# Two plain pairs ahead of the Strassen pairs, and a down-projection with five raw weight buffers, an in-place activation split and PSUM banks that rotate over its groups

## The chip, the cores and the metric

The kernel runs on one core of one Trainium2 chip. Its metric is the device time of one execution in microseconds (us); less is better. Times of whole runs are medians of several runs. The profile is one execution taken by the hardware profiler.

## The reference

One inference step of a two-layer encoder over 1024 prompt positions and 8 x 16 sample positions, 1152 rows of 1024 values in float32. Each layer has an attention block and a feed-forward block (ConvFFN), both modulated by vectors computed from c and closed by a layer norm. Layer 0 uses sliding-window attention, layer 1 a chunk band with its own bias table and a K/V projected after layer 0. The part that the change touches is the feed-forward block and the norm after it:

```python
def conv_ffn(h, prev, w_up, conv_w, conv_b, w_down):
    u = h @ w_up                                   # 1024 -> 2 x 2816
    ...
    ue = jnp.concatenate([prev.astype(u.dtype), u], axis=1)
    y = conv_b
    for tap in range(CONV_W):                      # causal depthwise, 3 taps
        y = y + conv_w[tap] * ue[:, tap:tap + T]
    a, g = jnp.split(y, 2, axis=-1)
    out = (jax.nn.gelu(g) * a) @ w_down            # 2816 -> 1024
    return out, ue[:, T:]
...
x = layer_norm(DEEPNORM_ALPHA * x + (1 + g_f) * f, ln_g[l, 1], ln_b[l, 1])
```

## The kernel before, in words

Every float32 matmul is done as three float32r matmuls: each operand is split into a high part (a copy with rounding, on ScalarE, L160) and a low part (the rest, a subtraction on VectorE or GpSimd, L171). H holds the high and low part of the transposed layer input for all 1152 rows (nine tiles of 128). X1 and X2 hold work operands, F is a float32 arena of 12672 columns whose regions are reused by hand, `ws` are two raw weight buffers, `wslots` four slots for split weights. PSUM has eight banks of 512 columns.

The program is written in program order against a scheduler that lays out each engine's instructions ahead of time, by a simulated timeline and with program order as priority. At run time each engine runs its own list in that order, and waits on semaphores where an operand or a buffer is not ready; SyncE (SP) issues all the loads and stores from one list. `self.bg` is background work (the ada vectors of later blocks), advanced by step().

One layer is attention(), out_proj(), ffn(), and at its end down().

*out_proj()* goes over the tiles 8, 0, ..., 7, writes the new transposed input of a tile to H and to hD in DRAM. Its last tiles use hf, xr, tmp, lng and lnb in F.

*ffn()* computes 22 pairs of 128 columns (one of the value half, one of the gate half). The first NPL pairs are *plain*: mmT() for each half and each of three column blocks, 24 matmuls a block, into banks `ub`, with the taps (conv_block) read from PSUM; L1032 copies the last rows of a block. All others are *Strassen pairs* (spair): seven products of half-size operands in place of eight, 24 matmuls each (L1180), read out of PSUM by L1139, L1142 and L1147 into rows `us` of F, on which conv_row() does the taps (L1058, L1019). The weight sums S1, S2, S3 lie at F[0:1536] and are made on GpSimd (L1129 to L1132). Both kinds end in gated(), which stores actD[j]. The rows y come from a ring of three at F[10492], F[6396] and F[7548].

The Strassen products need combined inputs: combine() loads hD tile by tile through a ring of buffers in F, makes the differences on GpSimd (L1087, L1088) and VectorE (L1089, L1090) and splits them into T2, T3, T4 (in X1 and X2); T1S is a float32 region at F[2706:5010], split into H by first(). The first product of a pair needs only H, the second T2, the fourth T3, the fifth T1. During the pairs the raw weights go through `wide`, a ring of the two ws buffers, F[11644:12668] and F[8700:9724]; in layer 0 the background ada loads go through the same ring, and their matmuls (L217) write bank 7.

*down()* computes three groups of three tiles (GR). For each j of 22, fetch() loads a weight row block (L175), splits it into a slot (four slots in layer 0, ten in layer 1, where H is free), loads 384 columns of actD[j] (L1237) into one of three raw buffers at F[0:1152], and splits them into one of twelve slots in X1. mm() adds 6 matmuls per tile (L1246) in banks 2i and 2i+1. tail() multiplies by the gate (L1260, the only reader of the banks), adds the residual loaded by L946, and normalises; in layer 0 the tile is transposed (L904) into banks 6 and 7, scaled (L912, L916), saved (L920) and split into H. Ahead of it layer 0 builds a bias table for layer 1 (tables_b) and writes its skewed copy with one store, skb (skew, L1317). ln_consts() loads the gates and the layer-norm rows, four loads of 512 KB.

The down-projection of layer 0 is followed by attention(1), which begins with vproj(1, 0): nine tiles in the order 0, 1, 2, 6, 7, 8, 3, 4, 5, 24 matmuls each (L302), in banks 0, 1, 2, 3 in turn. rescale() (L801) uses lng and lnb after that.

Of the kernel before, what the change touches and what calls it, by code (L numbers as in the profile page):

```python
# [10 lines left out]
F32 = mybir.dt.float32  # L11
# [21 lines left out]
NPL = 1  # L33
BGU = 0.5
# [62 lines left out]
class Trunk:  # L97
# [742 lines left out]
    def ln_consts(self, l, i):  # L840
        nc = self.nc
        g = self.gd[2 * l + i]
        nc.sync.dma_start(self.gateP, bass.AP(g.tensor, g.offset, [[0, 128], [1, D]]))
        nc.sync.dma_start(self.gateS, bass.AP(g.tensor, g.offset + D, [[D, 8], [0, 16], [1, D]]))
        ln = (2 * l + i) * 2
# [137 lines left out]
    def ffn(self, l, xsrc, xdst, affs):  # L983
# [29 lines left out]
        ub = Ring([0, 1, 2])  # L1013
# [65 lines left out]
        def combine():  # L1079
            ring = Ring([F[:, 1536:2560], F[:, 7548:8572]])  # L1080
            for t in (8, 0, 1, 2, 3, 4, 5, 6, 7):
# [41 lines left out]
        def spair(j):  # L1123
# [46 lines left out]
            for i, (src, q, g, start) in enumerate(plan):  # L1170
# [19 lines left out]
                self.step(BGU)  # L1190
# [20 lines left out]
    def down(self, l, xsrc, xdst, affs):  # L1211
# [10 lines left out]
        self.ln_consts(l, 1)  # L1222
        raw = Ring([F[:, i * 384 : i * 384 + 384] for i in range(3)])
# [6 lines left out]
        tb = Ring([6, 7])  # L1230
# [3 lines left out]
        def fetch(j, t0):  # L1234
            w = self.wload(I["wdn"][l, j])
            s = raw.next()
            nc.sync.dma_start(s, self.actD[j][:, t0 * 128 : t0 * 128 + 384])  # L1237
            a = acts.next()
            self.split(s, *a, "a", "v")
            return w, a  # L1240

        def mm(j, w, a, i):
            for hf in range(2):
                ps = self.bank(2 * i + hf)
# [9 lines left out]
        def tail(t, i):  # L1254
            row, sm = z.next(), self.sm.next()
            x = self.residual(t, xsrc, xr)
            gate = self.gateP if t < 8 else self.gateS
            for hf in range(2):
                n = slice(hf * 512, hf * 512 + 512)
                nc.vector.tensor_mul(row[:, n], self.bank(2 * i + hf), gate[:, n])  # L1260
# [19 lines left out]
        for gi, g in enumerate(GR):  # L1280
            keep = KEEP if l and gi == 2 else 0
            for j in range(NFF - keep):
                w, a = fetch(j, g[0])
                for i in range(3):
                    mm(j, w, a, i)
            if gi == 0:
                aff = affs()
            kept = [(j, *fetch(j, g[0])) for j in range(NFF - keep, NFF)]
            for i, t in enumerate(g):
                for j, w, a in kept:  # L1290
                    mm(j, w, a, i)
                tail(t, i)
        if not l:
            self.wring = Ring(ws)
# [277 lines left out]
```

## Time and profile before

| | |
|---|---|
| median of 3 runs | 2967.39 us (2963.93 to 2974.32) |
| the profiled execution | 2964.33 us, its span 2962.6 us |
| TensorE (PE) busy | 2743.6 us, 93% of the span |
| PE weight loads (PEld) busy | 2432.2 us, 82% |
| VectorE (DVE) busy | 1894.1 us, 64% |
| ScalarE (ACT) busy | 1298.4 us, 44% |
| GpSimd (POOL) busy | 1138.2 us, 38% |
| moved by DMA | 471.17 MB, 159 GB/s on average |
| mean granted TensorE clock | 0.965 |

How to read the rows that follow: in a timeline each row gives the start in us, the duration in us, the engine, the line of the kernel, the operation, what it writes and reads, the shape and a count of instructions merged into the row; the bracket is the idle time of that engine just before, and who ended it. `SPq` is a load or store being issued. Rows of the chain of waits give start, length and what the time went to. Rows that start with a window A:B give its length, then busy time and instruction count of PE, PEld, DVE, ACT and POOL, the granted clock, the DMA engines' share and GB/s.

### The profile page before, as it was taken

To read this page: it belongs to the slowest core of one execution; us is meant where nothing else is said; L and a number is where in the kernel's file an instruction comes from. 1 tells how busy PE (TensorE), PEld (TensorE's weight loads), DVE (VectorE), ACT (ScalarE), POOL (GpSimd) and SP (SyncE) were. 2 spreads that over 40 slices of the span, in tenths; PEclk is the share of its full clock that TensorE was granted. 3 is DMA by queue.
4 is the path that set the end of the run, shared out by engine and by line. 5 is a ranking of instruction groups with operands and counts; after the bars stand their busy time and mean duration, and the time that the engine had idled before them with its cause. 6 is when DMAs were issued, how large, how long until landed. Compare 5 with 4: busy or idle time off the path is not lost.

```text
span 2962.6 us, 47567 instructions
## 1 busy us (share of the span) xinstructions
PE 2743.6 (93%) x17782; PEld 2432.2 (82%) x17782; DVE 1894.1 (64%) x3702; ACT 1298.4 (44%) x2625; POOL 1138.2 (38%) x765
## 2 busy tenths in 40 slices
PE   7999899799999969999998999889889999998987
PEld 5888677699999957778998888758789999986766
DVE  4476777677777756672113677668768877865773
ACT  3466634333333333443325666652434444443442
POOL 2122523334433335664730111322433443336553
PEclk9999899899999989999999999999989999999999
DMA  8654454334444475665964457674422222155552
GB/s 292 206 176 149 151 177 163 122 129 139 137 132 137 128 253 174 220 209 169 299 219 151 125 157 194 185 207 150 150 81 75 67 85 75 53 184 175 191 192 86
DMA packets 221064, 471.17 MB, mean 159 GB/s; under 512 B 39616, under 2 KB 115600, under 8 KB 220832
## 3 DMA queue, kind: packets, MB, share of 16 engines
q1 hardware_dynamic: 220832, 468.13, 49.4%
q8 instruction: 140, 2.29, 0.3%
q14 instruction: 92, 0.75, 0.1%
HBM read 366.74 MB, written 110.74 MB: 161 GB/s over the span
## 4 chain that ended last, share of the span: by engine, by line
PE 67%; DMA 8%; DVE 5%; issue 3%; ACT 2%; POOL 2%; SPq 1%; POOLq 0%; ACTq 0%; DVEq 0%
PE PS L1180 30%; PE PS L1246 13%; PE PS L302 9%; PE PS L290 8%; DMA ws<-in_wdn_dram 3%; PE PS L564 1%; PE PS L586 1%; PE PS L217 1%; DVE xa L171 1%; DMA F<-actD 1%; PE PS L536 1%; POOL H L171 1%; PE PS L539 1%; POOL wl L171 1%; PE PS L904 1%
## 5 line engine op out<-in xcount | busy, mean ns | idle before, releaser
L171 POOL TENSOR_TENSOR wl<-ws,wh 128x1024 fp32r<-128x1024 f32 x136 | 336.5, 2481 | 384.8 <-ACT wh L160 357.0
L1180 PE MATMUL PS<-H,wh 128*128 128x256 f32 (+1 forms) x2688 | 414.3, 297 | 0.0
L171 DVE TENSOR_TENSOR xa<-F,xa 128x384 fp32r<-128x384 f32 (+1 forms) x168 | 271.6, 1628 | 208.2 <-ACT xa L160 196.7
L1246 PE MATMUL PS<-wh,xa 128*128 128x512 f32 x1128 | 362.7, 400 | 39.1 <-ACT wh L160 23.8
L160 ACT CAST wh<-ws 128x1024 fp32r<-128x1024 f32 (+1 forms) x232 | 203.6, 879 | 420.8 <-DMA ws<-in_wdn_dram 152.9
L1180 PEld LDWEIGHTS PS<-H,wh 128*128 128x128 f32 x2688 | 379.3, 191 | 0.0
L1142 DVE TENSOR_TENSOR F<-PS,F 128x320 f32<-128x320 f32 (+2 forms) x630 | 202.3, 351 | 142.2 <-PE PS L1180 139.0
L1246 PEld LDWEIGHTS PS<-wh,xa 128*128 128x128 f32 x1128 | 214.2, 190 | 93.0 <-ACT wh L160 24.6
L1019 DVE SCALAR_TENSOR_TENSOR F<-F 128x1024 f32<-128x1024 f32 x336 | 264.8, 826 | 35.7 <-ACT F L1058 35.4
L1180 PE MATMUL PS<-H,wl 128*128 128x320 f32 (+1 forms) x1344 | 244.0, 301 | 27.6 <-ACT H L160 25.0
L290 PE MATMUL PS<-H,wh 128*128 128x384 f32 (+1 forms) x1344 | 262.2, 340 | 0.0
L160 ACT CAST wh<-F 128x512 fp32r<-128x512 f32 x202 | 124.1, 622 | 278.8 <-PE PS L1180 169.7
L171 DVE TENSOR_TENSOR wl<-F,wh 128x512 fp32r<-128x512 f32 x202 | 201.4, 1004 | 58.1 <-ACT wh L160 57.8
L290 PEld LDWEIGHTS PS<-H,wh 128*128 128x128 f32 x1344 | 236.9, 191 | 1.4 <-issue 1.0
L1180 PEld LDWEIGHTS PS<-H,wl 128*128 128x128 f32 x1344 | 200.4, 192 | 43.5 <-ACT H L160 25.7
L1246 PE MATMUL PS<-wl,xa 128*128 128x512 f32 x564 | 225.5, 400 | 5.0 <-POOL wl L171 4.8
L1180 PE MATMUL PS<-xa,wh 128*128 128x320 f32 (+1 forms) x1344 | 207.4, 297 | 0.2 <-DVE xa L171 0.2
L1028 POOL TENSOR_TENSOR F<-F 128x16 f32<-128x16 f32 x88 | 39.8, 453 | 410.3 <-DVE F L1019 336.2
L1180 PEld LDWEIGHTS PS<-xa,wh 128*128 128x128 f32 x1344 | 189.4, 190 | 0.6 <-DVE xa L171 0.6
L1246 PE MATMUL PS<-H,xa 128*128 128x512 f32 x684 | 167.1, 405 | 20.5 <-DVE F L1260 13.2
L302 PE MATMUL PS<-wh,H 128*128 128x256 f32 (+1 forms) x936 | 170.3, 311 | 7.1 <-DVE H L171 3.8
L1246 PEld LDWEIGHTS PS<-H,xa 128*128 128x128 f32 x684 | 132.2, 194 | 54.2 <-issue 13.6
(242 smaller groups left out, 5516.2 us busy)
## 6 DMA issues: line engine op xcount, KB each, us to landing
ws<-in_wdn_dram SPq DMA_DIRECT2D x132, 512.0 KB
ws<-in_adaw_dram SPq DMA_DIRECT2D x62, 512.0 KB
F<-in_adaw_dram SPq DMA_DIRECT2D x50, 512.0 KB
ws<-in_wup_dram SPq DMA_DIRECT2D x50, 512.0 KB
actD<-F SPq DMA_DIRECT2D x44, 576.0 KB
F<-actD SPq DMA_DIRECT2D x132, 192.0 KB
F<-in_wup_dram SPq DMA_DIRECT2D x38, 512.0 KB
xa<-kH SPq DMA_DIRECT2D x60, 256.0 KB
```

The source lines that it names most:

```text
L160: nc.scalar.copy(out, in_)
L171: self.eng(el).tensor_sub(lo, src, hi.bitcast(F32))
L217: mm = nc.tensor.matmul(ps[32 * j : 32 * j + 32, hf * 256 : hf * 256 + 256], self.cT[:, k * 32 : k * 32 + 32], w[:, j * 256 : j * 256 + 25 ...
L290: self.nc.tensor.matmul(out[:, 0:n], w[a][:, k * 128 : k * 128 + 128], H[:, p, k, s0 : s0 + n], start=i == 0, stop=i == 23)
L302: self.nc.tensor.matmul(out[:, 0:n], H[:, p, j * kn + k, t0 : t0 + 128], w[a][:, k * n : k * n + n], start=i == 0, stop=i == 23,)
L536: mm = nc.tensor.matmul(o, q, khi[a][:, kc], start=first, stop=False, **kw)
L539: nc.tensor.matmul(o, q, klo[a][:, kc], start=False, stop=True, **kw)
L1019: nc.vector.scalar_tensor_tensor(o, u, cw[:, cc, i : i + 1], o, op0=ALU.mult, op1=ALU.add)
L1028: nc.gpsimd.tensor_add(y3[:, :, 0:2], y3[:, :, 0:2], E4[:, cc])
L1142: nc.vector.tensor_add(d, o, x)
L1180: nc.tensor.matmul(ps[:, 0:m], w[a][:, k * 128 : k * 128 + 128], x(p, k, n), start=start and c == 0, stop=c == 11, skip_group_check=True,)
L1246: nc.tensor.matmul(ps, a[p][:, i * 128 : i * 128 + 128], w[q][:, hf * 512 : hf * 512 + 512], start=j == 0 and c == 0, stop=j == NFF - 1 an ...
```

## The change

NPL goes from 1 to 2, so each layer has two plain pairs and 20 Strassen pairs; the plain blocks rotate over six banks. combine() uses a ring of three buffers, two of them from `wide`, and takes tile 8 as the sixth. Background work advances one step on each even product, four steps a pair, for half a step on each of seven.

In down(), F[0:1024] and two more regions join the raw weight ring: lng and lnb in layer 0, hf in layer 1 (five and four buffers). The raw activations are loaded into the low half of their slot and split there. The banks of a group are given by GB, those of its transposes by TBG. In groups without kept steps all three tiles are evicted ahead of the tails. The gates are loaded after the matmuls of j = 1, the ln rows with them in layer 1 and at the end of the stage in layer 0.

```diff
-NPL = 1
-BGU = 0.5
+GB = ((6, 7, 0, 1, 2, 3), (4, 5, 6, 7, 0, 1), (2, 3, 4, 5, 6, 7))
+TBG = ((2, 3), (0, 1), (0, 1))
+NPL = 2
...
-        ub = Ring([0, 1, 2])
+        ub = Ring([0, 1, 2, 3, 6, 7])
...
-            ring = Ring([F[:, 1536:2560], F[:, 7548:8572]])
-            for t in (8, 0, 1, 2, 3, 4, 5, 6, 7):
+            ring = Ring([F[:, 1536:2560], F[:, 8700:9724], F[:, 11644:12668]])
+            for t in (0, 1, 2, 3, 4, 8, 5, 6, 7):
...
-                self.step(BGU)
+                if i % 2 == 0:
+                    self.step(1)
...
-        self.ln_consts(l, 1)
-        raw = Ring([F[:, i * 384 : i * 384 + 384] for i in range(3)])
+        narrow = self.ws
+        self.ws = Ring(narrow.items + [F[:, 0:1024]] + ([self.hf] if l else [self.lng, self.lnb]))
...
-            s = raw.next()
-            nc.sync.dma_start(s, self.actD[j][:, t0 * 128 : t0 * 128 + 384])
-            a = acts.next()
-            self.split(s, *a, "a", "v")
-            return w, a
-
-        def mm(j, w, a, i):
+            hi, lo = acts.next()
+            raw = lo.bitcast(F32)
+            nc.sync.dma_start(raw, self.actD[j][:, t0 * 128 : t0 * 128 + 384])
+            self.copy("a", hi, raw)
+            nc.vector.tensor_sub(lo, raw, hi.bitcast(F32))
+            return w, (hi, lo)
+
+        def mm(j, w, a, gi, i):
             for hf in range(2):
-                ps = self.bank(2 * i + hf)
+                ps = self.bank(GB[gi][2 * i + hf])
...
-        def tail(t, i):
-            row, sm = z.next(), self.sm.next()
-            x = self.residual(t, xsrc, xr)
+        def evict(t, gi, i):
+            row = z.next()
             gate = self.gateP if t < 8 else self.gateS
             for hf in range(2):
                 n = slice(hf * 512, hf * 512 + 512)
-                nc.vector.tensor_mul(row[:, n], self.bank(2 * i + hf), gate[:, n])
+                nc.vector.tensor_mul(row[:, n], self.bank(GB[gi][2 * i + hf]), gate[:, n])
+            return row
+
+        def tail(t, gi, row):
+            x = self.residual(t, xsrc, xr)
             if l == 0:
                 nc.vector.scalar_tensor_tensor(row, x, ALPHA, row, op0=ALU.mult, op1=ALU.add)
-                self.norm_tail(t, row, xdst, aff, True, tb, "a", None, None, hfr, EL, VA)
+                self.norm_tail(t, row, xdst, aff, True, Ring(TBG[gi]), "a", None, None, hfr, EL, VA)
                 return
+            sm = self.sm.next()
...
                 for i in range(3):
-                    mm(j, w, a, i)
+                    mm(j, w, a, gi, i)
+                if gi == 0 and j == 1:
+                    self.ln_gates(l, 1)
+                    if l:
+                        self.ln_rows(l, 1)
...
+            rows = []
             for i, t in enumerate(g):
                 for j, w, a in kept:
-                    mm(j, w, a, i)
-                tail(t, i)
+                    mm(j, w, a, gi, i)
+                if kept:
+                    tail(t, gi, evict(t, gi, i))
+                else:
+                    rows.append(evict(t, gi, i))
+            for t, row in zip(g, rows):
+                tail(t, gi, row)
+        self.ws = narrow
         if not l:
+            self.ln_rows(l, 1)
             self.wring = Ring(ws)
```

ln_gates() and ln_rows() are the two halves of ln_consts(): the two gate loads, and the two loads of layer-norm rows.

More of the change, by code (lines that the diff above doesn't have):

```diff
@@ L840, in ln_consts, with ln_gates @@
     def ln_consts(self, l, i):
+        self.ln_gates(l, i)
+        self.ln_rows(l, i)
+    def ln_gates(self, l, i):
         nc = self.nc
@@ L844, in ln_consts, with ln_rows @@
         nc.sync.dma_start(self.gateS, bass.AP(g.tensor, g.offset + D, [[D, 8], [0, 16], [1, D]]))
+    def ln_rows(self, l, i):
+        nc = self.nc
         ln = (2 * l + i) * 2
@@ L1229, in down @@
         self.wring = Ring(order)
-        tb = Ring([6, 7])
         hfr = Ring([self.hf])
```

## The prediction

> **What bounds the kernel now.** I read the page first (busy shares, chain by engine), then the idle time of PE in order of time, then the other engines around each hole.
>
> ```profile
> span 2962.6 us, 47567 instructions
> PE 67%; DMA 8%; DVE 5%; issue 3%; ACT 2%; POOL 2%; SPq 1%; POOLq 0%; ACTq 0%; DVEq 0%
> 2133.00:2628.00 495.00, 476.11 (x3528) 474.88 (x3529) 380.58 (x653) 210.54 (x379) 193.60 (x155) 0.97 0.25 79
> 2628.00:2948.00 320.00, 285.21 (x1191) 227.30 (x1189) 188.29 (x183) 119.04 (x163) 172.45 (x71) 0.94 0.53 172
> ```
>
> The chain is two thirds matmul. In the Strassen stage of layer 1 (third line) PE is busy 476.11 of 495 us, so its pairs are PE time and nothing else; the down-projection (fourth line) leaves 35 us of 320 empty. So the change can pay only where PE stands still: before and at the start of the Strassen pairs, and in the down-projection. These are its stops there, PE's timeline, with the wait and who ended it in brackets:
>
> ```profile
> 511.24 2.95 PE L290 MATMUL PS<-H,wl 128*128 128x388 f32 x8 [5.99 <-ACT F L1032]
> 529.74 0.97 PE L217 MATMUL PS<-ws,C 128*32 128x256 f32 x8 [3.05 <-DMA ws<-in_adaw_dram]
> 533.53 1.44 PE L1180 MATMUL PS<-xa,wl 128*128 128x320 f32 x4 [2.82 <-ACT xa L160]
> 550.07 2.29 PE L1180 MATMUL PS<-H,wl 128*128 128x320 f32 x8 [13.07 <-ACT H L160]
> 1076.13 2.93 PE L1246 MATMUL PS<-wh,xa 128*128 128x512 f32 x6 [14.83 <-ACT wh L160]
> 1103.87 2.93 PE L1246 MATMUL PS<-wh,xa 128*128 128x512 f32 x6 [8.95 <-ACT wh L160]
> 2125.12 2.95 PE L290 MATMUL PS<-H,wl 128*128 128x388 f32 x8 [6.48 <-ACT F L1032]
> 2133.98 1.28 PE L1180 MATMUL PS<-H,wl 128*128 128x320 f32 x4 [1.78 <-DVE wl L171]
> 2147.94 1.44 PE L1180 MATMUL PS<-xa,wl 128*128 128x320 f32 x4 [5.78 <-ACT xa L160]
> 2164.02 2.29 PE L1180 MATMUL PS<-H,wl 128*128 128x320 f32 x8 [11.93 <-ACT H L160]
> 2663.58 0.79 PE L1246 MATMUL PS<-H,xa 128*128 128x512 f32 x1 [5.71 <-ACT H L160]
> 2666.00 14.24 PE L1246 MATMUL PS<-H,xa 128*128 128x512 f32 x52 [1.63 <-POOL H L171]
> 2744.51 0.76 PE L1246 MATMUL PS<-wh,xa 128*128 128x512 f32 x1 [13.63 <-DVE F L1260]
> 2852.16 8.16 PE L1246 MATMUL PS<-H,xa 128*128 128x512 f32 x23 [13.17 <-DVE F L1260]
> ```
>
> Entry to the pairs: 24.9 us in layer 0, 26.0 in layer 1. Down-projection: 23.8 in layer 0, 34.1 in layer 1. After a stop PE also runs slowly for a while: the six 512-wide matmuls at 1076.13 took 2.93 us, where 54 in a steady stretch take 12.76 (row in part 2), 1.42 for six; a restart there costs 1.5.
>
> **Part 1, the second plain pair.** Its price is plain time less Strassen time.
>
> ```profile
> 2100.53 1.58 PE L290 MATMUL PS<-H,wl 128*128 128x388 f32 x8
> 2104.78 1.58 PE L290 MATMUL PS<-H,wl 128*128 128x384 f32 x8
> 2164.02 447.64 PE PS L1180 x3345
> 504.88 1.12 POOL L1087 TENSOR_TENSOR F<-F 128x256 f32<-128x256 f32 x1 [2.34 <-issue]
> 547.15 0.72 POOL L1087 TENSOR_TENSOR F<-F 128x256 f32<-128x256 f32 x1 [5.55 <-DMA F<-hD]
> ```
>
> One block of a plain pair is 2104.78 - 2100.53 = 4.25 us, six make 25.5. The third line (chain of waits) gives 447.64 / 3345 x 168 = 22.5 us for a Strassen pair. So each layer pays 3.0 us more of PE. What it covers is combine(), which runs from the first to the last of its POOL subtractions above, 504.88 to 547.15, and whose last tile waited 5.55 us for its hD load behind a ring of two. The first subtraction cannot come sooner, since T1S lies over hf and xr, which the last out_proj tile still uses. With two plain pairs PE has 12 x 4.25 = 51 us of work from 480.8, so to about 535 with the transposes in between; the first Strassen product needs no combined operand and adds 22.5 / 7 = 3.2. T2 must then be complete at 538. At the old pace the last tile is done near 551, which leaves 13 us of wait; with three buffers filling each other's load time it may be done before 538, which leaves 0. The plain pair's own taps also take DVE time, so I take 6 us, and 1.5 for the slow restart. Six PSUM banks for the plain blocks remove the 5.99 and 6.48 us waits on L1032. Restarts before: the layer-1 pairs had 495 - 21 x 22.5 = 22.5 us beyond PE work, against 17.7 us of waits after 2133.98, so about 5; the eight matmuls at 2125.12 lost 2.95 - 1.58 = 1.4 more. Gain: 26 + 6.5 - 3 - 7.5 = 22 in layer 1, and the same taken for layer 0, together **44** (ends 24 and 60: the 6 us at 13 with a longer restart, or at 0).
>
> The tile order of combine() changes only which half is ready first, at no cost. step(1) on the even products makes 4 background steps a pair for 3.5: the same loads in fewer pairs, taken at nothing (its cover is the pairs' PE time; the price if that is gone is a rival below).
>
> **Part 2, down-projection of layer 1.** The two boundary waits are not missing PSUM but a queue:
>
> ```profile
> 2733.25 2.39 DVE L171 TENSOR_TENSOR xa<-F,xa 128x384 fp32r<-128x384 f32 x1 [4.64 <-ACT xa L160]
> 2741.37 2.39 DVE L171 TENSOR_TENSOR xa<-F,xa 128x384 fp32r<-128x384 f32 x1 [1.09 <-ACT xa L160]
> 2743.68 1.27 DVE L1260 TENSOR_TENSOR F<-PS,F 128x512 f32<-128x512 f32 x2
> 2741.00 2.34 POOL L171 TENSOR_TENSOR H<-ws,H 128x1024 fp32r<-128x1024 f32 x1 [1.14 <-ACT H L160]
> 2645.11 12.76 PE L1246 MATMUL PS<-H,xa 128*128 128x512 f32 x54
> ```
>
> PE ended group 0 at 2730.9; its eviction (L1260) stands in DVE's order behind the splits of the next fetches, each waiting for a weight load. Fetches come about every 4 us (three splits from 2733.25 to 2741.37, the first and the last shown), while a step of j takes 18 x 12.76 / 54 = 4.25 us of PE, so prefetch never gets ahead. With four raw buffers (ws twice, F[0:1024], hf) the loads overlap, and the next limit is POOL's split, 2.34 us, and DVE beside it, 2.39: some 2.7 us. Gaining 1.5 us a step over 22 steps, the fetches run up to the ten weight slots, and the evictions stand behind nothing late. Rotating banks add little by themselves: two free banks are 6 matmuls, 1.4 us, just the 1.27 us of one token's eviction. Boundaries fall from 13.63 + 13.17 to about 1 each (ends 0 and 3), with 1.5 us of restart saved at each. Entry: moving the gate and ln loads behind j = 1 puts 2 MB behind more weights; hf becomes free after the last ua row, before j = 3 is due. So 7.3 falls to about 1. Gain 24.8 + 3 + 6.3 = **34** (ends 20, the fetches catching up only in the second group, and 37).
>
> **Part 3, down-projection of layer 0.** Here the entry is a transfer:
>
> ```profile
> 1045.83 0.61 SPq L1317 DMA_DIRECT2D skb<-eb  x1
> 1048.81 21.18 DMA F<-actD
> skb<-eb SPq DMA_DIRECT2D x1, 6144.0 KB
> 1060.31 1.53 DVE L1019 SCALAR_TENSOR_TENSOR F<-F 128x1024 f32<-128x1024 f32 x2
> ```
>
> The skew of the layer-1 table, 6144 KB, is issued at 1045.83; a 192 KB load issued 3 us later took 21.18 us. tables_b() writes into us[0]. With 21 Strassen pairs us[0] is free during the last pair; with 20 it is the last pair's gate row, read by taps that began at 1060.31. So the skew starts about 20 us later, 6 us after PE enters the down-projection. The weights of j = 3 and 4 go to lng and lnb, which lie under the last yg and are free only once actD[21] is stored, also after the skew starts. j = 0 to 2 cover 12.8 us; then PE waits till the skew has passed, about 20 us (ends 12 and 28). The second stop, 8.95, I put down to the 2 MB of gate and ln loads ahead of the weights; half of it is moved to the end and the rest meets weights already loaded, so it goes. Both old stops with restart cost 23.8 + 3; the new one 20 + 1.5. Gain **5** (ends -3 and 13). On SP the actD store, the gates and those two weights are queued behind the skew, and PE waits for the last. The ln rows, moved to the end of the stage, are awaited only by rescale() on POOL, and that waits for zd anyway (2.98 us in the L801 row of part 4): no cost; without that cover they delay only POOL work that no matmul awaits until the next out_proj.
>
> By the Trainium skill's "DMA: Bandwidth & Descriptors", section "Queues, rings and completion order", completion is not first-in first-out per issuing engine; on each DMA engine descriptors start in ring order. The 21.18 us row looks like the ring order; by the first half alone small loads could pass the skew (rival 4).
>
> **Part 4, the join of the layers.** This is a wait the change adds. The last group's transposes now use banks 0 and 1 (TBG), and the V-projection that follows takes banks 0, 1, 2, 3 in turn.
>
> ```profile
> 1382.06 0.64 PE L302 MATMUL PS<-wh,H 128*128 128x256 f32 x4
> 1396.22 1.03 PE L904 MATMUL PS<-C,F 128*128 128x128 f32 x8
> 1404.34 2.13 PE L904 MATMUL PS<-C,F 128*128 128x128 f32 x8 [3.98 <-ACT F L920]
> 1415.08 1.03 PE L904 MATMUL PS<-C,F 128*128 128x128 f32 x8
> 1418.27 1.09 ACT L920 COPY F<-PS 128x512 f32<-128x512 f32 x2
> 1388.78 1.12 PE L302 MATMUL PS<-wh,H 128*128 128x256 f32 x8
> 1389.73 0.64 PE L302 MATMUL PS<-wl,H 128*128 128x256 f32 x4
> 1411.66 2.40 POOL L801 TENSOR_TENSOR F<-F 128x1024 f32<-128x1024 f32 x1 [2.98 <-DMA F<-zd]
> ```
>
> Before, PE went straight from the down-projection into L302 at 1382.06 and put the three tails' transposes (L904) between. Now the first V tile must wait until the last tail has left bank 0, which before was near 1419, 37 us after. The first transposes came 14 us after 1382.06, the others 8.1 and 10.7 us apart. Without the V evictions beside them I estimate 7 apart, and with the reads of the last the banks are free after about 30. In that time PE has only the tiles on banks 2 and 3, 24 x (1389.73 - 1388.78) / 8 = 2.9 us each, and three times 1.03 of transposes: 21 us idle against 3.98 before. Loss **17** (ends 5, the tails in half their time, and 27, no faster than before and a restart). On PE everything of the second attention stands behind it.
>
> **Sum.** 44 + 34 + 5 - 17 = 66 us. The profiled execution took 2964.33 us (span 2962.6); less 66 it is 2898. The median of the runs, 2967.39, is 3 us above it, so I forecast **2901**. All bad ends together leave 24 + 20 - 3 - 27 = 14 gained, 2953; all good ones 60 + 37 + 13 - 5 = 105, 2862.
>
> **Rivals.**
> 1. *The second pair hides nothing.* combine() is written behind plain(1), so DVE and POOL may do it after plain(1)'s taps, and its ring now takes two of the Strassen weight buffers. Then each entry keeps its waits and pays 3 us: 66 - 44 - 6 = 16 gained, **2951**. For: the old waits end on ACT and DVE, not PE. Against: POOL is idle 5.55 us there, for a load.
> 2. *Evictions behind a deeper queue.* If the order is laid out for ten fetches ahead but loads stay near 4 us, an eviction stands behind seven late fetches, 28 us, instead of 13.4; two of them cost 29 more: 66 - 34 - 29 = 3, **2964**. For: 704 KB every 2.7 us is 260 GB/s, and this stage moved 172 on average (fourth line of the first fence). Against: 172 is what two buffers ask for; the skew's 6144 KB, read and written in about 24 us (1045.83 to 1069.99), show that some 260 GB/s each way can be moved.
> 3. *Slower: the layer-0 pair loop.* A ring of four buffers now serves 2 weights and 4 background loads a pair. If these loads come late (the 3.05 us at 529.74 is such a wait), PE stops in each of 18 pairs. It decides from (66 + 9) / 18 = 4.2 us a pair; at 6 it costs 108, **3009**. Against: with 5.5 loads a pair PE shows no such stop between 550.07 and the end of the pairs.
> 4. *The skew holds nothing back.* If loads issued after it pass it, j = 3 is late only by its own load, about 3 us, and part 3 gains 17 more: **2884**. Against: the 21.18 us row.
> 5. *The change does not do what it says:* only four raw buffers in layer 1, and two of the five in layer 0 are late; part 3 already counts that.
>
> **How the numbers follow.** Forecast 0.60, rival 1 0.12, rival 2 0.12, rival 3 0.08, rival 4 0.08. Runs before spread over 10 us in 2967, so 0.3%, 9 us, is about what a measurement can tell. Faster: 0.60 + 0.08 + 0.10 of rival 1 + 0.04 of rival 2 = 0.82; same: 0.01 + 0.03 = 0.04; slower: 0.14. The range goes from 2858, just past the forecast's best end (rival 4 reaches lower only with it), to 2952, which takes in rival 1; above it lie rivals 2 and 3, at 0.20.
>
> **What would show it.** Right: no wait on L1032 before the plain blocks; the wait for H L160 in the pairs under 8 us; L1260 ending no wait over 3 us in layer 1; the skew issued after the last pair and a stop of some 20 us on j = 3; a stop of some 20 us ahead of L302 between the layers. Wrong: waits of 10 us or more still at L1180's start, at L1260, or repeated inside the layer-0 pairs.

## The result: 2894 us against 2968, ratio 0.975

The changed kernel takes **2894.11 us** (median of 4 runs, 2890.53 to 2900.63); the kernel before, run beside it, 2968.48 (4 runs, 2963.93 to 2974.32). The ratio is 0.9751, 95% interval [0.9726, 0.9776]. The forecast was 2901. The profiled execution took 2892.5 us, 71.8 less than the 2964.33 of before.

The page of the changed kernel, span and chain:

```profile
span 2890.7 us, 47351 instructions
PE 80%; DMA 8%; DVE 5%; ACT 3%; issue 2%; POOL 2%; SPq 0%; POOLq 0%; DVEq 0%; ACTq 0%
```

The chain was 67% PE and is now 80%. PE's timeline of the changed kernel shows what is left of the stops in the stages that the change touches (all over 0.7 us; at the join of the layers, those of its first 60 us):

```profile
541.25 0.73 PE L1188 MATMUL PS<-xa,wl 128*128 128x256 f32 x4 [1.40 <-ACT xa L161]
545.79 0.86 PE L1188 MATMUL PS<-H,wl 128*128 128x320 f32 x4 [2.31 <-ACT F L1155]
1083.09 2.92 PE L1255 MATMUL PS<-wh,xa 128*128 128x512 f32 x6 [33.44 <-ACT wh L161]
1366.11 1.97 PE L912 MATMUL PS<-C,F 128*128 128x128 f32 x8 [5.20 <-DVE F L902]
1377.01 1.97 PE L912 MATMUL PS<-C,F 128*128 128x128 f32 x8 [8.93 <-ACT F L928]
1381.12 1.22 PE L303 MATMUL PS<-wh,H 128*128 128x256 f32 x4 [2.15 <-POOL H L172]
1387.59 0.74 PE L303 MATMUL PS<-wh,H 128*128 128x256 f32 x4 [1.03 <-POOL H L172]
2139.04 0.73 PE L1188 MATMUL PS<-xa,wl 128*128 128x256 f32 x4 [0.77 <-ACT xa L161]
2144.15 0.86 PE L1188 MATMUL PS<-H,wl 128*128 128x320 f32 x4 [2.87 <-ACT F L1155]
2606.88 2.93 PE L1255 MATMUL PS<-wh,xa 128*128 128x512 f32 x6 [7.15 <-ACT wh L161]
2628.12 12.18 PE L1255 MATMUL PS<-H,xa 128*128 128x512 f32 x51 [1.92 <-POOL H L172]
```

L1188 is the Strassen matmul (L1180 before), L1255 the down-projection (L1246), L912 the transposes of its tails (L904), L303 the V-projection (L302). Gone are the two waits on the convolution ahead of the pairs, the 13 and 12 us waits in them, and both boundary stops of layer 1 (no L1268, the eviction, ends a wait). Two stops are larger or new: 33.44 us at the entry of layer 0's down-projection, and 5.20 + 8.93 + 2.15 + 1.03 = 17.3 at the join of the layers. The same by windows. The columns are the window, its length, busy time of PE, PEld, DVE, ACT and POOL, granted clock, DMA share, GB/s. First before, the down-projections of layer 1 and layer 0:

```profile
2628.30:2947.40 319.10, 284.91 (x1188) 227.01 (x1186) 187.69 (x183) 119.04 (x163) 171.92 (x71) 0.94 0.53 172
1061.30:1382.20 320.90, 290.48 (x1239) 230.20 (x1239) 174.52 (x186) 121.46 (x178) 184.05 (x76) 0.96 0.61 201
```

Then the changed kernel, the down-projections of layer 1 and layer 0 and the pair loops of layer 0 and layer 1:

```profile
2587.10:2876.00 288.90, 279.57 (x1189) 223.24 (x1187) 160.48 (x183) 115.70 (x159) 173.91 (x69) 0.99 0.54 183
1037.00:1355.20 318.20, 284.76 (x1239) 229.32 (x1238) 134.54 (x181) 119.81 (x171) 180.68 (x75) 0.95 0.59 200
550.00:1037.00 487.00, 487.00 (x3813) 452.42 (x3812) 343.73 (x602) 191.41 (x342) 204.69 (x147) 1.00 0.42 146
2148.00:2587.00 439.00, 439.00 (x3295) 439.00 (x3294) 351.74 (x593) 193.37 (x343) 181.66 (x138) 1.00 0.26 84
```

PE is busy for all of both pair loops. The account by stages, each from PE's timeline, in us. The bounds are the start of the first 388-column plain matmul, the end of the last Strassen matmul, the end of the last down-projection matmul, the first 388-column plain matmul of layer 1, and so on:

| stage | before | changed | gain | forecast |
|---|---|---|---|---|
| plain and Strassen pairs, layer 0 | 575.4 | 549.7 | 25.7 | 22 |
| down-projection, layer 0 | 320.9 | 318.1 | 2.8 | 5 |
| join, second attention and its out-projection | 718.3 | 730.6 | -12.3 | -17 |
| plain and Strassen pairs, layer 1 | 527.7 | 501.4 | 26.3 | 22 |
| down-projection, layer 1 | 319.1 | 288.8 | 30.3 | 34 |
| sum | | | 72.8 | 66 |

What lies ahead of the first stage cost 1.4 and what lies behind the last gained 0.5; that makes 71.9 us, for 71.8 between the profiled executions.

### The profile page after: what moved, and what is told of

The parts are those of the page before. It is cut to its first block, busy times and chain, and to the rows that moved or that the text cites. A ratio compares the mean times of both kernels' runs of the same rounds, so it can differ in the third digit from the quotient of the medians.

```text
span 2890.7 us, 47351 instructions
## 1 busy us (share of the span) xinstructions
PE 2725.0 (94%) x17734; PEld 2425.9 (84%) x17734; DVE 1805.0 (62%) x3674; ACT 1296.9 (45%) x2613; POOL 1157.0 (40%) x761
## 4 chain that ended last, share of the span: by engine, by line
PE 80%; DMA 8%; DVE 5%; ACT 3%; issue 2%; POOL 2%; SPq 0%; POOLq 0%; DVEq 0%; ACTq 0%
PE PS L1188 31%; PE PS L1255 17%; PE PS L291 11%; PE PS L303 10%; PE PS L587 2%; PE PS L565 2%; PE PS L218 2%; PE PS L537 1%; PE PS L540 1%; DMA actD<-F 1%; DMA F<-in_wdn_dram 1%; DMA ws<-in_wo_dram 1%; DVE F L504 1%; PE PS L912 1%; POOL H L172 1%
## 5 line engine op out<-in xcount | busy, mean ns | idle before, releaser
L1255 PE MATMUL PS<-wh,xa 128*128 128x512 f32 x1128 | 359.0, 397 | 40.6 <-ACT wh L161 40.6
L1188 PE MATMUL PS<-H,wh 128*128 128x256 f32 (+1 forms) x2560 | 394.2, 296 | 0.0
L1188 PEld LDWEIGHTS PS<-H,wh 128*128 128x128 f32 x2560 | 360.3, 190 | 0.0
L1248 DVE TENSOR_TENSOR xa<-xa 128x384 fp32r<-128x384 f32 x132 | 185.7, 1419 | 238.0 <-ACT xa L161 238.0
L172 POOL TENSOR_TENSOR wl<-ws,wh 128x1024 fp32r<-128x1024 f32 x87 | 216.8, 2495 | 291.5 <-ACT wh L161 277.5
L161 ACT CAST wh<-F 128x512 fp32r<-128x512 f32 (+1 forms) x249 | 176.0, 713 | 347.4 <-PE PS L1188 139.7
L291 PE MATMUL PS<-H,wh 128*128 128x384 f32 (+1 forms) x1536 | 294.8, 338 | 0.0
L1255 PEld LDWEIGHTS PS<-wh,xa 128*128 128x128 f32 x1128 | 213.3, 189 | 93.5 <-ACT wh L161 41.5
L161 ACT CAST wh<-ws 128x1024 fp32r<-128x1024 f32 (+1 forms) x175 | 146.8, 843 | 247.9 <-PE PS L1188 99.7
L1027 DVE SCALAR_TENSOR_TENSOR F<-F 128x1024 f32<-128x1024 f32 x320 | 249.7, 822 | 6.4 <-ACT F L1066 5.3
L1188 PE MATMUL PS<-H,wl 128*128 128x256 f32 (+1 forms) x1280 | 228.1, 298 | 5.2 <-ACT F L1155 5.2
L1255 PE MATMUL PS<-wl,xa 128*128 128x512 f32 x564 | 224.8, 399 | 0.2 <-POOL wl L172 0.2
L1188 PEld LDWEIGHTS PS<-H,wl 128*128 128x128 f32 x1280 | 189.4, 190 | 12.2 <-issue 5.8
L1188 PE MATMUL PS<-xa,wh 128*128 128x256 f32 (+1 forms) x1280 | 196.1, 295 | 0.6 <-DVE xa L172 0.6
L303 PE MATMUL PS<-wh,H 128*128 128x256 f32 (+1 forms) x936 | 171.3, 313 | 11.2 <-DVE H L172 4.0
L1188 PEld LDWEIGHTS PS<-xa,wh 128*128 128x128 f32 x1280 | 178.7, 188 | 1.4 <-DVE xa L172 1.0
L172 POOL TENSOR_TENSOR wl<-F,wh 128x1024 fp32r<-128x1024 f32 x53 | 130.4, 2463 | 91.7 <-ACT wh L161 89.5
L1255 PE MATMUL PS<-H,xa 128*128 128x512 f32 x684 | 161.6, 395 | 1.9 <-POOL H L172 1.9
```

The source lines that it names most:

```text
L161: nc.scalar.copy(out, in_)
L172: self.eng(el).tensor_sub(lo, src, hi.bitcast(F32))
L291: self.nc.tensor.matmul(out[:, 0:n], w[a][:, k * 128 : k * 128 + 128], H[:, p, k, s0 : s0 + n], start=i == 0, stop=i == 23)
L303: self.nc.tensor.matmul(out[:, 0:n], H[:, p, j * kn + k, t0 : t0 + 128], w[a][:, k * n : k * n + n], start=i == 0, stop=i == 23,)
L1027: nc.vector.scalar_tensor_tensor(o, u, cw[:, cc, i : i + 1], o, op0=ALU.mult, op1=ALU.add)
L1188: nc.tensor.matmul(ps[:, 0:m], w[a][:, k * 128 : k * 128 + 128], x(p, k, n), start=start and c == 0, stop=c == 11, skip_group_check=True,)
```

## The experiments

Each is the changed kernel with the edit that is shown, run in 4 executions beside the kernel before; a ratio is to the kernel before, and the changed kernel's own is 0.9751. The stretch ahead of the first bound of the table, which no edit touches, is 484.7 us (e5) to 496.7 us (e9) long in these traces, and 487.3 in the changed kernel's; so the parts are read by the stages of the table, and not by totals alone. Four questions: what is the 33.44 us stop, what is the 17.3, which part of the edit pays at the pairs, which in the down-projection.

**e1: the skew inside layer 0's pairs.**

```
+            if l == 0 and j == 10:
+                self.tables_b(us.next()[:, 2:1170])
+                self.skew(1)
             spair(j)
...
-            self.tables_b(F[:, 1152:3200])
-            self.skew(1)
```

> The changed kernel, with the bias table of layer 1 built and its skewed 6144 KB copy stored during the Strassen pairs of layer 0 (before the pair j = 10, in one of the us buffers) and not at the start of the down-projection. Theory A (the 33.4 us stop of PE ahead of the fourth weight block of layer 0 is the skew, which all later loads queue behind): the stop falls under 6 us, no new stop in the pairs, the whole at 2866 us (2860 to 2874). Rival B (the stop is the two weight buffers under the last yg row, lng and lnb, that come free late in any case, and 1 MB of gate loads): the stop stays at 15 us or more, the whole at 2878 or above.

Measured: 2894.04 us, ratio 0.9734 [0.9707, 0.9761]. The time is unchanged, but the trace is not. At the down-projection the stop fell to 13.45 us (first row, PE's timeline); two new stops stand in the pairs, the first of them begun some 22 us after the store was issued at 731.06:

```profile
1082.20 2.93 PE L1257 MATMUL PS<-wh,xa 128*128 128x512 f32 x6 [13.45 <-ACT wh L161]
758.59 1.08 PE L218 MATMUL PS<-ws,C 128*32 128x256 f32 x8 [5.65 <-DMA ws<-in_adaw_dram]
765.76 1.44 PE L1188 MATMUL PS<-H,wl 128*128 128x320 f32 x4 [4.82 <-DVE wl L172]
```

The down-projection is 20.3 us shorter and layer 0's pairs 13.2 longer. Neither expectation was met: the stop lies between theirs. So 20 of the 33.44 us are the skew, which in one piece holds up loads in both places; the 13.45 remain without it. The chain through them in e1 runs through the last actD store and the weights for lng and lnb, which lie under the buffers that this store reads:

```profile
1066.99 3.24 DMA actD<-F
1070.25 10.78 DMA F<-in_wdn_dram
```

**e8: the skew on ScalarE's queue**, at its place in the program.

```
-        self.nc.sync.dma_start(
+        (self.nc.scalar if l else self.nc.sync).dma_start(
```

> The changed kernel with the skew of the layer-1 table issued by ScalarE on its own DMA queue instead of SyncE's, at the same place of the program. Theory A (the loads stood behind the skew's descriptors in SyncE's ring): the weights of j = 3 and the actD[21] store pass it, the stop on j = 3 falls from 33.4 to 10 to 16 us, where the late lng and lnb buffers remain, and the kernel takes 2870 to 2880. Theory B (the 16 DMA engines themselves are kept busy by the 6 MB, whatever the queue): the stop stays over 25 us, 2890 to 2897. Between: shared by turns, the stop falls by about half of the skew's 20 us, 2882 to 2887.

Measured: 2887.26 us, ratio 0.9726 [0.9699, 0.9753]: the case in between, 0.3 us past the end of its range. The stop is 24.71, 8.7 less. While both queues have work (the DMA view of 1057 to 1071) SyncE's q1 and ScalarE's q10 take about equal shares of the 16 DMA engines (packets, MB, share):

```profile
q1 hardware_dynamic: 811, 2.67, 52.1%
q10 hardware_dynamic: 840, 2.58, 49.3%
```

From 1071 to 1080.2, when q1 has little to move, q10 has 67.6% and q1 11.1%. The chain has the skew itself at 29.94 us:

```profile
1050.27 29.94 DMA skb<-eb
```

So it lands at 1080.21, and PE's stop had ended at 1077.30. The load into lng, which that stop waited for, was issued at 1059.88 (1071.72 in the changed kernel) and could be split at 1076.20: it started 11.8 us earlier and took 16.3 us against 10.20. Another queue lets the loads share, not pass.

**e2: K and V of layer 1 without banks 0 and 1.**

```
-        kvb = Ring(list(SB[l]))
+        kvb = Ring([[0, 1, 2, 3], [2, 3, 4, 5, 6, 7]][l])
```

> The changed kernel, with the K and V projections at the start of layer 1 rotating over banks 2 to 7, so that none of them shares banks 0 and 1 with the last group's transposes. Theory A (the stops of 5.2, 8.9, 2.1 and 1.0 us at the join of the layers are V tiles waiting for banks 0 and 1): they fall to 5 us together, the whole 12 us lower, 2882 (2878 to 2887). Rival B (they are ScalarE's list, where the load of the layer input for attention stands ahead of the tails, so the tails are late whatever the banks): less than 4 us lower, 2890 or above.

**e3: no rotation of the banks.**

```
-GB = ((6, 7, 0, 1, 2, 3), (4, 5, 6, 7, 0, 1), (2, 3, 4, 5, 6, 7))
-TBG = ((2, 3), (0, 1), (0, 1))
+GB = ((0, 1, 2, 3, 4, 5),) * 3
+TBG = ((6, 7),) * 3
```

> The changed kernel, with the PSUM banks of before: every group in banks 0 to 5, transposes in 6 and 7. Theory A (the boundary waits went with the four and five raw weight buffers; rotating the banks gains 1.4 us a boundary at most and costs the wait at the join): boundaries under 3 us each, the stops at the join back to some 5 us, the whole 8 to 12 us lower, 2884 (2880 to 2889). Rival B (the rotation is what removed the boundary waits): L1255 waits for the eviction for 8 us or more at each boundary of layer 1, the whole 2900 or above.

Measured: e2 2876.84 us, ratio 0.9679 [0.9652, 0.9706]; e3 2886.15, ratio 0.971 [0.9684, 0.9736]. In e2 one stop of 3.52 us is left at the join (PE's timeline, first row), in e3 one of 3.78; no L303 waits in either:

```profile
1379.68 1.66 PE L912 MATMUL PS<-C,F 128*128 128x128 f32 x8 [3.52 <-ACT F L928]
```

The 17.3 us come from the shared banks. (Two of the four rows are transposes that wait for the tails' own work, two are V tiles that wait for POOL's split of H; that the sharing is behind them, e2 and e3 show by taking it away.) e2's median is 1.2 us below its range. The stage from the join to the next pairs is 706.4 us in e2 and 715.0 in e3, against 730.6. In e3 both down-projections keep their length (318.2 and 288.2) and have no boundary stop: the rotation gave nothing there and cost the join. The 12 us by which e2's stage lies below that of the kernel before (718.3) were not foreseen. Of the 24.2 us to the changed kernel, 13.8 are these stops, and 7.5 a shorter busy time of PE in the stage (671.32 to 663.78); why six banks for K and V shorten it was not taken apart.

**e4: one plain pair**, NPL = 1.

> The changed kernel with one plain pair instead of two, the six banks, the ring of three in combine and the down-projection left as they are. Theory A (the second plain pair is the cover for combine): waits for ACT at the start of the Strassen pairs come back, 12 us or more a layer (24 in all, plus restarts), less 3.0 us a layer of PE time; the skew is early again, so the stop of 33.4 us falls to some 15 and gives back about 18; the whole within 8 us of the changed kernel, 2894 (2886 to 2904). Rival B (the third combine buffer and the six banks did it, the pair itself only costs): entry waits stay under 5 us a layer, the whole at 2872 or below.

Measured: 2921.5 us, ratio 0.9828 [0.98, 0.9855]. The pairs take 11.8 us more in layer 0 and 13.8 in layer 1, which is theory A. The stops at the entry come to 13.5 and 14.7 us, against 24.9 and 26.0 before, so the other edits of this stage must hold the rest. The total lies 18 us above the range all the same: the skew is early again, issued 16 us before the pairs end, but the down-projection of layer 0 is only 4.5 us shorter (313.6), not 18. Stops of 7.51 and 18.35 stand there in place of the 33.44; the second ends with weights in F whose load was issued at 1078.76, after the last actD store (1074.58).

**e5: combine()'s ring of two.**

```
-            ring = Ring([F[:, 1536:2560], F[:, 8700:9724], F[:, 11644:12668]])
+            ring = Ring([F[:, 1536:2560], F[:, 8700:9724]])
```

> The changed kernel with combine()'s ring back at two buffers (F[:, 1536:2560], F[:, 8700:9724]), all else kept. Theory A (the prediction's part 1: three buffers fill each other's load time, worth the 5.55 us that the last tile waited for its load before): the first Strassen products of each layer wait some 5 to 10 us more, each layer's pairs (first plain matmul to last Strassen matmul) grow by that, 2904 to 2914 us. Theory B (the second plain pair covers the loads whatever the ring): under 1.5 us a layer, 2891 to 2897.

**e6: three banks for the plain blocks**, ub = Ring([0, 1, 2]).

> The changed kernel with ub = Ring([0, 1, 2]) for the plain blocks, all else kept. Theory A (the prediction's part 1: six banks remove one wait of about 6 us on the convolution's row and 1.4 of restart in each layer): a wait of 4 to 6 us on the convolution returns ahead of the plain blocks, some of it two or three times now that there are two plain pairs, 2904 to 2920 us. Theory B (what PE waits there it would have waited at the first Strassen product, where T2 is late by 3.7 us anyway): under 2 us a layer, 2892 to 2899.

**e12: the old tile order and background step.**

```
-            for t in (0, 1, 2, 3, 4, 8, 5, 6, 7):
+            for t in (8, 0, 1, 2, 3, 4, 5, 6, 7):
...
-                if i % 2 == 0:
-                    self.step(1)
+                self.step(0.5)
```

> The changed kernel with combine()'s tiles in the old order (8, 0, 1, ..., 7) and step(0.5) on every product in place of step(1) on the even ones, all else kept. Theory A (the prediction's part 1: both at no cost): each layer's pairs stay within 2 us of 549.7 and 501.4, 2890 to 2898 us. Theory B (with tile 8 late, the 5-tile half is ready one load earlier, and that was part of the gain): the first Strassen products wait 2 to 6 us more in each layer, 2899 to 2907; if only layer 0 grows, it is the step.

Measured: e5 2905.5 us, ratio 0.9784 [0.9763, 0.9806]; e6 2906.53, 0.9788 [0.9759, 0.9817]; e12 2902.4, 0.9769 [0.9749, 0.9789]. In layer 1 a stop on a combined operand is back in e5 (its PE timeline):

```profile
2154.60 2.29 PE L1188 MATMUL PS<-H,wl 128*128 128x320 f32 x8 [7.00 <-ACT H L161]
```

In e6 there is one ahead of a plain block, a little under the 4 to 6 us expected, and a longer one at the entry to the Strassen products (its PE timeline):

```profile
2124.92 2.90 PE L291 MATMUL PS<-H,wl 128*128 128x384 f32 x8 [3.71 <-POOL F L1096]
2143.55 1.22 PE L1188 MATMUL PS<-xa,wl 128*128 128x256 f32 x4 [4.28 <-ACT xa L161]
```

Without the ring of three the pairs are 3.5 us (layer 0) and 12.0 (layer 1) longer, where 5 to 10 were expected in each, with three banks 6.3 and 6.0. In e6 the trace puts the plain block's wait down to POOL's L1096, a subtraction of combine(), and not to the convolution as before. e12's trace has the pairs at 548.8 and 501.8 us, so both edits are worth nothing there, as forecast; but its median is 8 us above the changed kernel's and falls in theory B's range. The two intervals overlap, and its profiled execution took 2893.84; whether those 8 us are real stays open.

**e7: two raw weight buffers**, self.ws = Ring(list(narrow.items)) in down().

> The changed kernel with only the two usual raw weight buffers in the down-projection (self.ws = Ring(list(narrow.items))), its in-place activation split and rotating banks kept. Theory A (the prediction's part 2: the fetches are held to one load in about 4 us by the two raw buffers, and the evictions stand behind them on DVE): both boundary stops of layer 1 are back with 9 to 14 us each, its down-projection is 308 to 320 us long against 288.8, 2912 to 2927. Theory B (the activation split in place, without its ring of three, was what freed the fetches): no stop over 3 us at a boundary, down-projection of layer 1 under 294, 2890 to 2900.

**e9: e7 with the old activation ring as well.**

```
+        raws = Ring([F[:, i * 384 : i * 384 + 384] for i in range(3)])
...
-            raw = lo.bitcast(F32)
+            raw = raws.next()
             nc.sync.dma_start(raw, ...)
-            self.copy("a", hi, raw)
-            nc.vector.tensor_sub(lo, raw, hi.bitcast(F32))
+            self.split(raw, hi, lo, "a", "v")
```

> The changed kernel with both parts of the old fetch: two raw weight buffers as in e7, and the activations loaded through a ring of three 384-column buffers at F[:, 0:1152] and split from there, not in place. Rotating banks, the order (all three evictions, then the tails) and the moved gate and ln loads stay. e7 left 6.60 and 6.12 us of the old boundary stops of 13.63 and 13.17 in layer 1. Theory A (the in-place activations, twelve buffers instead of three, took the other half): the stops are back at 11 to 15 us each, layer 1's down-projection is 308 to 318 us, 2908 to 2920. Theory B (the other half went with the order of evictions and the banks): the stops stay at 5 to 8 us, down-projection 298 to 302, 2895 to 2902.

Measured: e7 2898.08 us, ratio 0.9752 [0.9727, 0.9777]; e9 2923.77, 0.9829 [0.9799, 0.986]. The boundaries of layer 1, PE's timeline of e7 (two rows) and of e9 (two rows):

```profile
2688.59 0.80 PE L1255 MATMUL PS<-wh,xa 128*128 128x512 f32 x1 [6.60 <-DVE F L1268]
2789.93 10.31 PE L1255 MATMUL PS<-H,xa 128*128 128x512 f32 x36 [6.12 <-DVE F L1268]
```

```profile
2708.30 0.79 PE L1255 MATMUL PS<-wh,xa 128*128 128x512 f32 x1 [11.22 <-DVE F L1268]
2816.89 3.35 PE L1255 MATMUL PS<-H,xa 128*128 128x512 f32 x7 [14.23 <-DVE F L1268]
```

e7 missed both of its expectations: the stops come back at half their size, and layer 1's down-projection is 299.9 us, between 288.8 and 319.1. (Its total is that of theory B only because layer 0 gained, below.) e9 shows the other half: with three activation buffers the stops are nearly whole again, 25.5 us together for 26.8 before, at 314.4 us. (Its total is 4 us above theory A's range; the stretch ahead of the pairs is 9.4 us longer in its trace.) SyncE's waits tell why. In e9's down-projection of layer 1 (2595 to 2910) it stood with an activation load in hand until DVE had split its raw buffer:

```profile
SPq L1247 <- DVE xa L172: 94.9, 32, 4.5
```

The kernel before has the same wait (121.5 us, 40 times), and e7 has none. Four raw weight buffers with three activation buffers were not run. Two more things show in e7. Layer 0's down-projection is 13.2 us *shorter* (304.9), its stop 19.84: with no weights in lng and lnb only the skew is left, which agrees with e1 from the other side. And at the entry of layer 1 the 7.15 + 1.92 us are 1.45 + 1.92: the wait on j = 3 came with its raw buffer. The entries of layer 0 (first row) and layer 1 in e7's PE timeline:

```profile
1091.27 2.93 PE L1255 MATMUL PS<-wh,xa 128*128 128x512 f32 x6 [19.84 <-ACT wh L161]
2613.37 0.50 PE L1255 MATMUL PS<-H,xa 128*128 128x512 f32 x1 [1.45 <-ACT H L161]
2615.79 4.61 PE L1255 MATMUL PS<-H,xa 128*128 128x512 f32 x13 [1.92 <-POOL H L172]
```

**e10: the skew cut into 16 stores of 384 KB**, and two raw buffers in layer 0.

```
+            if l == 0 and j == 3:
+                self.tables_b(us.next()[:, 2:1170])
+            if l == 0 and 4 <= j < 20:
+                self.skew_head(j - 4)
             spair(j)
...
-        self.ws = Ring(narrow.items + [F[:, 0:1024]] + ([self.hf] if l else [self.lng, self.lnb]))
+        self.ws = Ring(narrow.items + ([F[:, 0:1024], self.hf] if l else []))
```

> The changed kernel with the skew cut into 16 stores of 384 KB, one ahead of each pair j = 4 to 19 of layer 0 (its table built ahead of j = 3), and in layer 0 only the two usual raw buffers in the down-projection; layer 1 as in the changed kernel. If the 33.4 us stop is 20 of the skew's one long transfer and 13.4 of loads into lng and lnb, as e1 and e7 have it: no stop over 4 us at the entry of layer 0's down-projection, its length 284 to 292 us as in layer 1, and no stop over 2 us in the pairs, since a 384 KB store holds a load back by about 1.3 us (20 / 16); 2862 to 2870 us. Rival (any store into the table ahead of the pairs' loads costs its time there, as e1's stops of 5.65 and 4.82): layer 0's pairs 8 to 16 us longer, 2872 to 2882.

**e11: e10, e2's banks, and hf as a raw buffer from j = 6 on.**

```
+        self.ws = Ring(narrow.items + [F[:, 0:1024]] * l)
...
+                if l and gi == 0 and j == 6:
+                    self.ws = Ring(self.ws.items + [self.hf])
                 w, a = fetch(j, g[0])
```

> e10 with e2's banks for K and V of layer 1 (2, 3, 4, 5, 6, 7), and in layer 1's down-projection the third and fourth raw buffers added in steps: F[:, 0:1024] from the start, hf only from j = 6, because in the changed kernel the weights of j = 3 waited for the last pair's row that lies over hf. If the three are independent: 17 less than e10 by the banks, 4 to 6 less by the entry of layer 1 (9.1 us of stops to 3.4, as in e7), boundaries still without stops; 2840 to 2850 us. If the join only trades its wait for the one of a later load, 10 us less than e10 or nothing.

Measured: e10 2869.62 us, ratio 0.9662 [0.9635, 0.9689]; **e11 2838.3 us, ratio 0.9549 [0.9517, 0.9581]**, which is less than both kernels. At the entry of layer 0's down-projection e10 has one stop over 0.9 us (last row of its PE timeline below), and its length is 285.1 us; the pairs are 4.5 us longer, with two stops of 1.93 and 2.26 near their start, a little more than the 2 us allowed:

```profile
571.99 0.41 PE L1188 MATMUL PS<-H,wl 128*128 128x320 f32 x1 [1.93 <-DVE F L1150]
574.66 1.43 PE L1188 MATMUL PS<-xa,wl 128*128 128x320 f32 x4 [2.26 <-DVE wl L172]
1077.59 0.51 PE L1258 MATMUL PS<-wl,xa 128*128 128x512 f32 x1 [1.93 <-POOL wl L172]
```

The stores did not go out one per pair. The program has one ahead of each of the pairs 4 to 19, but in SyncE's list, which is laid out ahead of time, all 16 were issued within 21 us, during the first two Strassen pairs, in three groups with loads between them (SyncE's timeline of e10):

```profile
554.35 1.86 SPq L1344 DMA_DIRECT2D skb<-eb  x3
557.84 6.65 SPq L1344 DMA_DIRECT2D skb<-eb  x6
568.03 7.06 SPq L1344 DMA_DIRECT2D skb<-eb  x7
```

What came between the groups did not wait for all 6144 KB: a weight load of e10, issued behind the first three, took 9.38 us, where in e1 the store issued 0.8 us behind the whole skew took 24.20 (chains of e10 and e1):

```profile
556.88 9.38 DMA F<-in_wup_dram
731.86 24.20 DMA actD<-F
```

So e10 shows a skew in pieces with loads between, early in the pairs. What one store per pair would cost, and how much of the difference to e1's 13.2 us is the earlier place, was not run.

e11 has 710.0 us from the join on (e10: 729.2), and a down-projection of layer 1 of 277.2 us without a stop over 0.9 us (e10: 288.1). Its two stops at the join (PE's timeline of e11):

```profile
1353.94 1.09 PE L912 MATMUL PS<-C,F 128*128 128x128 f32 x8 [1.17 <-DVE F L902]
1359.01 0.66 PE L912 MATMUL PS<-C,F 128*128 128x128 f32 x4 [2.55 <-ACT F L928]
```

The profiled executions of e10 and e11 differ by 22.9 us (2866.85 and 2843.96). That this is the sum of 17 and 6 that independence asked for is luck: the two edited stages gained 19.2 and 10.9, and others, which e11 left as in e10, were 7.2 longer. The medians differ by 31.3, and e11's lies 2 us below its range. e11's 10.9 us in the down-projection are e10's stop of 7.16, one of 1.55 behind it, and some 2 us more, most likely PE's slow running after them.

## Why the prediction was right, and where its terms were off

**Part 1, the entries.** Forecast 44, measured 52. The mechanism held: one plain pair more covers combine(), and e4 puts what it is worth, its 3.0 us of PE paid, at 11.8 and 13.8 us. Mis-sized was the remainder: 7.5 us were set aside per layer for a late T2 and a restart; the stops left are 1.40 + 2.31 in layer 0 and 0.77 + 2.87 in layer 1, in each layer one on T2 and one on a bank. The first of each pair is the second product's second half, waiting for ScalarE's split of T2 (`xa`), so T2 was late by 1.4 and 0.8 us; the other waits for ScalarE to copy a bank out (L1155). That the ring of three would fill the load time is shown by e5, the six banks' 6 us a layer by e6, tile order and step at nothing by e12. The single losses in layer 1 (13.8, 12.0, 6.0) sum to 31.8, more than the 26.3 together: the waits overlap, and what one edit removes another partly covered.

**Part 2, down-projection of layer 1.** Forecast 34, measured 30.3. That the stops were a queue on DVE and not missing PSUM is right: e3 leaves out the rotation and they do not return. But the step "with four raw buffers the loads overlap" named only half of the cause. e7 keeps two raw buffers and still loses half of each stop; it takes the three activation buffers too (e9) to bring them back. DVE's split of a fetch waits for its activations as well as its weights; twelve in-place buffers let SyncE issue those loads ahead (its 94.9 us of waits in e9, none in e7). The other edits of the stage bring at most 1.3 us to the boundaries by themselves: e9 keeps the rotation, the order of evictions and the moved gate loads, and its stops are 25.5 us of 26.8. Together the two kinds of buffer took the stops to zero, 2 us better than forecast. The entry was the bad term: 7.3 was to fall to 1, and 7.15 + 1.92 were measured. The prediction said that "hf becomes free after the last ua row, before j = 3 is due". It becomes free too late: SyncE waited for the taps of that row with the weight load in hand (waits of SyncE, 2560 to 2620, changed kernel), and e11, which uses hf from j = 6, has no such stop.

```profile
SPq L176 <- DVE F L1027: 4.3, 1, 4.3
```

By the Trainium skill's "Perfetto Trace Analysis", section "Matmuls", independent matmul groups should rotate through different PSUM banks, so that eviction overlaps the next group's matmuls. With two free banks at a boundary e3 shows no such gain here, and at the join the rotation cost 12 to 16 us.

**Part 3, down-projection of layer 0.** Forecast 5, measured 2.8, from two misses that nearly cancel, so the small error of the total is luck. The late skew is as predicted: issued at 1047.40, 10 us behind the last pair (6 were estimated), with what follows it on SyncE's queue held back.

```profile
1045.59 0.32 SPq L1337 DMA_DIRECT2D eb<-F  x1
1047.40 0.60 SPq L1342 DMA_DIRECT2D skb<-eb  x1
1048.13 6.88 SPq L1075 DMA_DIRECT2D actD<-F  x1
```

Those rows are SyncE's timeline. The chain of waits goes through the last of them:

```profile
1048.13 23.53 DMA actD<-F
1071.72 10.20 DMA F<-in_wdn_dram
```

But the stop was sized as the skew alone, 20 us. The weights for lng and lnb can only be *issued* once the actD store has passed. PE stood for 22.0 us until then, for 10.2 while they loaded, and 1.1 for ScalarE's split: 33.44 with the gaps between. The prediction had this dependence in its text and left its load time out of the sum. Against it stand 5.7 us less PE busy time (290.48 to 284.76) and 6.6 us of small stops that are gone (idle was 30.4, of which 23.8 were the two large ones; now it is 33.4, all of it the one stop). e9 against e7 gives 8.7 us of such gain to the in-place activations in this layer, which the prediction costed only for layer 1.

**Part 4, the join.** Forecast -17, measured -12.3. The bank conflict is shown by e2 and e3. The forecast stop of 21 us was 17.3: the down-projection ended at 1355.17, and the V tile after those that could run at once began at 1381.12, 26 us later instead of the 30 estimated.

**The rivals.** Rival 1 (no cover) falls with the entries' 3.7 us, rival 2 (evictions behind late fetches) with boundaries that have no stop. Rival 3 (stops in each layer-0 pair) falls with 487.00 busy of 487.00 us. Rival 4 (loads pass the skew) falls with the store issued 0.7 us after it, which landed 23.53 us later. Where the skew is on the same queue, the loads keep ring order; on ScalarE's (e8) they take turns. The Trainium skill's "DMA: Bandwidth & Descriptors", section "Queues, rings and completion order", says that each DMA engine goes round-robin between the queue rows that have work; the shares of 52.1% and 49.3%, while both had work, agree. Its other half, that completion is not first-in first-out, carried rival 4; no run here shows a load that passed the skew on the same queue. Rival 5 is the nearest to a hit: in layer 0 two of the raw buffers came too late to help, and without them (e7) the stage is 13 us shorter.

## What to carry to other kernels

A borrowed buffer is worth its bytes only from the moment its last reader is done: lng, lnb and hf joined the ring at its first turn, and each put its own release on the path of PE; adding hf some turns later (e11) was worth 10.9 us, and leaving the borrowed buffers out in layer 0 (e7) 13.2. When a stop is put down to a queue on an engine, list every load that the queued instruction waits for; taking away one of two causes took away half of the stop. Before moving a large store whole, cut it into pieces that let loads in between: moved whole into the pairs it cost them 13.2 of the 20.3 us that it saved (e1), in pieces 4.5 (e10). And look in the trace for where it was issued, since program order did not tell it.

## What was not expected of the hardware

A 6144 KB transfer in DRAM on its own queue does not run in the background: while SyncE's queue had loads too, each side got about half of the DMA engines, and it took 29.94 us (e8). In 16 pieces of 384 KB, issued within 21 us with loads between, it cost layer 0's pairs 4.5 us in all, against 13.2 in one piece at another place of the loop. And PE's busy time shrank with its stops: the 1188 or so matmuls of layer 1's down-projection took 284.91 us at a granted clock of 0.94 and 279.57 at 0.99, so 5.3 us of its gain are shorter busy time. That these are the matmuls which no longer follow a stop is argued, not shown; the prediction's 1.5 us a restart gave 3 for the two boundaries.
